# A decoder layer's tiles at other places in SBUF: split tiles 128 bytes longer, x sums and mixer weights 64 bytes into theirs, everything 32 bytes further on, and four small changes of order

## The chip, the cores and the metric

One core of a Trainium2 chip runs the whole layer in one launch. The metric is the device time of one execution in microseconds; where several runs of a kernel are compared, their median. A profiled execution gives the trace; its span is the time from the first to the last instruction.

## The reference

One decoder layer on a sequence of 512 tokens with 1,024 channels, all in float32 (batch 1, depth 1):

```python
x = x + 0.5 * rms_norm(swiglu_ffn(rms_norm(x, norm_pre[0]), ffn1_w_in, ffn1_w_out), norm_post[0])
mixed = token_mixer(rms_norm(x, norm_pre[1]), w_mix_in, ..., w_mix_out)   # HGRN2 + mLSTM heads
x = x + rms_norm(mixed, norm_post[1])
x = x + 0.5 * rms_norm(swiglu_ffn(rms_norm(x, norm_pre[2]), ffn2_w_in, ffn2_w_out), norm_post[2])

def swiglu_ffn(x, w_in, w_out):
    gate, up = jnp.split(x @ w_in, 2, axis=-1)
    return (jax.nn.silu(gate) * up) @ w_out          # 1024 -> 2 x 2816 -> 1024
```

The mixer is one projection to 3,592 columns, a causal convolution, two chunked recurrences and an output projection.

## The kernel before

**Split operands.** Every large matmul is done in float32r on operands split in two: `hi` is the operand rounded by a cast, `lo` the rest, and a product is three matmuls (hi·hi, hi·lo, lo·hi) into one PSUM bank. Weights come by DMA into `raw` tiles of 512 KB (queue of SyncE, L182); `split` (L184 to L212) casts one on ScalarE (L195: `hi`), subtracts on VectorE (L197: `lo`) into one of four `w` buffers, and then lets GpSimd add one raw block to another where a later product needs the sum (L209). `feed` (L214) splits ahead until four buffers are filled; the items stand in one list, so ScalarE, VectorE and GpSimd go through the splits in the list's order.

**The first half of each FFN** multiplies x (transposed, tokens as columns) by blocks of W_in in a scheme with seven block products instead of eight: for each of 11 column groups t the products p1 to p7, each 24 matmuls of 256 columns (`prod`, L444; the matmul is L456). p1, p2, p4 and p5 take x blocks as they are, in the tiles `xq`; p3, p6 and p7 take sums of x blocks, in three tiles of tag `s` (`sq`). Here the weights `w` are the stationary operand and the x blocks the moving one. What is done with a finished product is in `after` (L471): additions and silu on VectorE and ScalarE, between PSUM and the tile `hf` (L475, L483 to L489). t=0, and parts of t=1 and 2, are done early, while the other tokens are still being normalised: products c1 to c4 and e1 to e4, list `HEADS` (L41). c1, c3 and c4 use the `s` tiles for split weights before the sums go there (`stay`, L791). `ORDER` (L43 to L48) is the order of all products, written out by hand; it fixes TensorE's order and the list of splits.

**The second half of each FFN**, and the mixer's token-wise projections, are matmuls of 512 columns (`mm3`, L123 to L127): there the weights `w` are the moving operand, and the stationary one is a block of the hidden layer (`hs`, also tag `s`, from `h_tile`, L628; the last one lies in `xq3`) or of x (`xq`, `t_mm`, L719). Other mixer projections have `xq` moving, 256 columns, and `w` stationary (`in_k`, L405, L409; `head_mm`, L414, L419).

**Between the stages.** At the end of the mixer `mix_out1` finishes tokens in four blocks; `ffn_head` (L511) starts the second FFN in between: splits, copies, the transposes of the last blocks (`trans`), and `sums` (L271), which makes the x sums with a chain of small operations on ScalarE and VectorE (L277 for `lo` and subtractions, L278 for `hi`). `behind` holds instructions back until given ones have been issued. `start` (L543) does the same by hand for the first FFN. It begins with `gain_pe` (L101): a norm row is loaded, multiplied with ones on TensorE (L114) and copied to all partitions, while `spin` (L118) issues filler matmuls (3, then 4, then 4) where TensorE would wait.

**Where the tiles lie.** A tile's byte offset in its partition follows from the sizes of those allocated ahead of it (each rounded up to 32 bytes). What matters below is the offset modulo 128:

| tile | offset | modulo 128 |
|---|---|---|
| `nhalf`, 8 constants | 17024 | 0 |
| `xs` | 17056 | 32 |
| `xq0` to `xq3`, 8192 bytes each | 33440 and on | 32 |
| `w`, four of 8192 bytes | 87008 and on | 96 |
| tag `s` (`sq`, `hs`), three of 8192 bytes | 179936 and on | 96 |

Within these tiles the blocks of a matmul begin at multiples of 512 bytes, so the column holds for every operand. The 6,370 matmuls of the program contain, in float32r with 256 columns: 2,592 of `xq` on `w`, 288 of `xq` on weights in `sq`, 1,440 of sums in `sq` on `w`; with 512 columns: 1,008 of `w` on `hs` and 624 of `w` on `xq`.

Of the kernel before, what the change touches and what calls it, by code (L numbers as in the profile page):

```python
# [14 lines left out]
P = 128  # L15
T = 512
# [3 lines left out]
ND = D // P  # L20
NF = FF // P
EPS = 1e-6
RAW, WBUF = 3, 4
PAIRS = NF // 2
HALF = T // 2
KH = ND // 2
# [13 lines left out]
HEAD = 3  # L40
HEADS = [("c1", 0), ("c3", 0), ("c2", 0), ("c4", 0), ("p1", 1), ("e1", 0), ("e3", 0)]  # L41
HEADS += [("e2", 0), ("p1", 2), ("p2", 1), ("e4", 0), ("p2", 2)]
ORDER = HEADS + [(p, 1) for p in ("p7", "p5", "p3", "p6")] + [("p5", 2), ("p7", 2), ("p3", 2), ("p4", 1), ("p6", 2)]  # L43
for _t in range(HEAD, PAIRS):
    if _t == HEAD:
        ORDER += [("p1", _t), ("p3", _t), ("p5", _t), ("p4", _t - 1)] + [(p, _t) for p in ("p7", "p6", "p2")]
    else:
        ORDER += [("p1", _t), ("p4", _t - 1)] + [(p, _t) for p in ("p3", "p5", "p7", "p6", "p2")]  # L48

# [9 lines left out]
class Item:  # L59

    def __init__(self, key, loads, rows=None, adds=(), dst=None):
        self.key, self.loads, self.rows, self.adds, self.dst = key, loads, rows, adds, dst
        self.reads = {key, *(k for pair in adds for k in pair)}


class Layer:
    def __init__(self, ctx, tc, aps):
        self.tc, self.nc = tc, tc.nc  # L70
        self.__dict__.update(aps)
        nc = self.nc
        pool = lambda name, **kw: ctx.enter_context(tc.tile_pool(name=name, bufs=1, **kw))
        self.cp, self.wp, self.sp, self.psp = pool("cp"), pool("wp"), pool("sp"), pool("psp", space=PSUM)
        self.uid, self.hold = 0, ()

        self.ident = self.cp.tile([P, P], F32, name="ident")
        make_identity(nc, self.ident)
        self.nhalf = self.cp.tile([P, 8], F32, name="nhalf")
        nc.gpsimd.memset(self.nhalf, -0.5)  # L80
        self.xs = self.cp.tile([P, NT, D], F32, name="xs")

        self.xq = [self.cp.tile([P, 2, KH, HALF], F32R, name=f"xq{n}") for n in range(4)]
        self.prm = self.cp.tile([P, 36], F32, name="prm")
# [16 lines left out]
    def gain_pe(self, tag, row):  # L101

        nc = self.nc
        g = self.cp.tile([P, D], F32, tag=tag, bufs=1, name=self.nm(tag))
        r = self.hf[0:1, 14:16, :].rearrange("p a t -> p (a t)")
        nc.sync.dma_start(r, row)
        one = self.st("one", P)[:1]
        nc.gpsimd.memset(one, 1.0)
        self.spare = self.ps()
        self.spin(3)  # L110
        for h in range(2):
            ps = self.ps()
            v = slice(512 * h, 512 * h + 512)
            nc.tensor.matmul(ps, one, r[:, v], start=True, stop=True)  # L114
            nc.vector.tensor_copy(g[:, v], ps)
        return g
# [67 lines left out]
    def split(self):  # L184

        nc = self.nc
        it = self.items.popleft()
        raw = self.raw[it.key]
        _, a, b = raw.shape
        w = it.dst() if it.dst else self.wp.tile([P, 2, a, b], F32R, tag="w", bufs=WBUF, name=self.nm("w"))  # L190
        hi, lo = w[:, 0], w[:, 1]
        self.ready.append((w, it.dst is not None))
        rows = it.rows
        if rows is None:
            nc.scalar.copy(hi, raw)  # L195
            yield
            nc.vector.tensor_tensor(lo, raw, hi.bitcast(F32), op=ALU.subtract)  # L197
        else:
            for j in range(a):
                nc.scalar.activation(hi[:, j], raw[:, j], AF.Copy, scale=rows[:, j : j + 1])  # L200
            yield
            for j in range(a):
                nc.vector.scalar_tensor_tensor(
                    lo[:, j], raw[:, j], rows[:, j : j + 1], hi[:, j].bitcast(F32), op0=ALU.mult, op1=ALU.subtract
                )
        with self.behind(*self.hold):
            for out, other in it.adds:
                o, c = self.raw[out], self.raw[other]
                nc.gpsimd.tensor_tensor(o, o, c, op=ALU.add)  # L209
        self.load_due(self.done)  # L210
        self.done += 1
        yield  # L212

    def feed(self, most=WBUF):  # L214

# [55 lines left out]
    def sums(self, i, src):  # L271


        nc = self.nc
        v = slice((i % 2) * P, (i % 2 + 1) * P)
        f = [x[:, :, v] for x in self.xf]
        sub = lambda out, a, b: nc.vector.tensor_tensor(out, a, b, op=ALU.subtract)  # L277
        hi = lambda dst, src: nc.scalar.copy(dst[:, 0, :, v], src)  # L278
        lo = lambda dst, src: sub(dst[:, 1, :, v], src, dst[:, 0, :, v].bitcast(F32))
        p1, p0 = self.turn(src, 1), self.turn(src, 0)  # L280
        a22 = self.hf[:, 10 + i, :].rearrange("p (c t) -> p c t", c=KH)
        s1, s2, s3, s4 = self.xq[2], self.sq[2], self.sq[1], self.sq[0]
        hi(self.xq[2], p0)
        hi(self.xq[3], p1)
        nc.scalar.copy(a22, p1)
        lo(self.xq[2], p0)
        lo(self.xq[3], p1)
        yield
        sub(p1, p0, a22)
        sub(p0, f[0], p0)  # L290
        hi(s3, p0)
        lo(s3, p0)
        yield
        sub(p0, f[0], p1)
        hi(s1, p1)
        lo(s1, p1)
        yield
        hi(s2, p0)
        sub(p1, f[1], p0)
        lo(s2, p0)  # L300
        yield
        hi(s4, p1)
        lo(s4, p1)
        yield
# [127 lines left out]
    def open_ffn(self, ctx):  # L432

        hp = self.hpool = ctx.enter_context(self.tc.tile_pool(name=self.nm("hp"), bufs=1))
        self.hf = hp.tile([P, NF, T], F32, name=self.nm("hf"))
        self.xf = [self.hf[:, j : j + 2, :].rearrange("p a (b t) -> p (a b) t", t=HALF) for j in (NF - 4, NF - 2)]
        self.sq = [hp.tile([P, 2, KH, HALF], F32R, tag="s", bufs=3, name=self.nm("sq")) for _ in range(3)]
        self.left = {"p1": self.xq[0], "p2": self.xq[1], "p4": self.xq[3], "p5": self.xq[2], "p6": self.sq[2], "p7": self.sq[1], "p3": self.sq[0]}
        self.left.update({"c1": self.xq[0], "c2": self.xq[1], "c3": self.xq[0], "c4": self.xq[1]})
        self.left.update({"e1": self.xq[2], "e2": self.xq[3], "e3": self.xq[2], "e4": self.xq[3]})  # L440
        self.gs, self.held, self.copies = [], {}, []
        self.hs, self.bank, self.later, self.n, self.q, self.had = deque(), {}, deque(), {}, {}, set()
# [68 lines left out]
    def ffn_head(self, trans):  # L511
# [10 lines left out]
        with self.behind(*norm):  # L522
            for g in self.copies:
                next(g)
            self.feed()
        S = lambda: [next(g) for g in self.gs]
        then = {("e1", 0): S, ("e3", 0): S, ("e2", 0): S, ("e4", 0): S}
        for n, (p, t) in enumerate(HEADS):
            self.feed()
            self.lag()  # L530
            self.prod(p, t)
            self.after(p, t)
            if n == 0:
                with self.behind(*norm):
                    trans(2)
            elif n == 2:
                trans(3)
            elif (p, t) in then:
                then[p, t]()
# [3 lines left out]
    def start(self, norm, xn):  # L543
# [2 lines left out]
        norm(1)  # L546
        q = [[self.part(i, h, xn[i]) for h in range(2)] for i in range(2)]
        step = lambda *gs: [next(g) for g in gs]
        self.spin(4)
        step(q[0][0], q[0][1], q[0][0])  # L550
        self.spin(4)
        split = self.split()
        step(q[1][0], q[1][1])
        next(split)
# [72 lines left out]

    def h_tile(self, k2, dst=None):  # L628

        t = dst if dst is not None else self.hpool.tile([P, 2, 2, T], F32R, tag="s", bufs=3, name=self.nm("hs"))  # L630
        src = self.hf[:, 2 * k2 : 2 * k2 + 2, :]
        self.nc.scalar.copy(t[:, 0], src)
        self.nc.vector.tensor_tensor(t[:, 1], src, t[:, 0].bitcast(F32), op=ALU.subtract)  # L633
        return t
# [106 lines left out]
    def mix_items(self):  # L741
# [2 lines left out]

        def item(src, a, b, rows=None):
            key = ("mix", len(made))
            made.append(Item(key, [Load(key, src, a, b)], rows))

        def f(c0):
            for n in range(4):  # L750
# [14 lines left out]
    def ffn_items(self, name, w_in, w_out):  # L765
# [26 lines left out]
        for p, t in ORDER:  # L792
            if p[0] == "e":
                continue
            dst = (lambda n=stay[p]: self.sq[n]) if p in stay else None
            made.append(Item((name, t, place[p]), own.get((p, t), ()), None, adds.get((p, t), ()), dst))
        for h in range(2):
            for k2 in range(PAIRS):
# [585 lines left out]
def layer(tc, aps):  # L1384
    with ExitStack() as ctx:
# [26 lines left out]
        with ExitStack() as f1:  # L1412
            L.open_ffn(f1)
            with tc.manual_schedule():
                first = L.start_loads()
                for i in range(NT):
                    for h in range(2):
                        v = slice(512 * h, 512 * h + 512)
                        (nc.scalar if i == 1 else nc.sync).dma_start(L.xs[:, i, v], x[0, i * P : (i + 1) * P, v])
                        if i == h == 0:  # L1420
                            gp[0] = L.gain_pe("gpre", pre[0:1, :])
                    if i:
                        L.load(first.popleft())
                    if i == 1:
# [44 lines left out]
```

## Time and profile before

| | us |
|---|---|
| median of 3 runs | 976.48 (976.01 to 976.50) |
| the profiled execution | 976.29 |
| its span | 974.6 |
| TensorE busy | 960.6 |
| VectorE busy | 695.0 |
| ScalarE busy | 464.0 |
| GpSimd busy | 291.5 |

The profile's page lists busy time of the engines (PE is TensorE's matmuls, PEld its weight loads, DVE VectorE, ACT ScalarE, POOL GpSimd, SP SyncE), the chain of work that ended last, and groups of instructions by line: output<-inputs, shape, count, busy time and mean ns of one, then the idle time before them and what ended it. A timeline row gives start, duration from the first start to the last end, engine, line, tiles and count; in square brackets stands the idle time just before and what released it. The granted clock of TensorE is 0.997 in the mean. By stages: up to 14 us the start, to 92 us the first products, the first FFN to 374 us, the mixer to 627 us, the second FFN to 968 us, then the last norm and the stores.

### The profile page before, as it was taken

The numbers are of one execution on the slowest core, as the hardware profiler recorded it, in microseconds if no ns is written. First come the engines' busy times: TensorE is split into PE (matmuls) and PEld (weight loads), VectorE is DVE, ScalarE is ACT, GpSimd is POOL, SyncE is SP. The second block draws the span as 40 slices with busy tenths as digits, with TensorE's granted clock in tenths as the row PEclk, the third lists the DMA queues.
The fourth block names the chain that finished last, engine by engine and source line by source line (L and its number), as shares of the span: only waits on it lengthen the run. The fifth ranks groups of instructions, "written<-read, shape, count | busy, mean of one in ns | idle before, by whom it ended". The sixth has DMA issues, their size and how long they took to land.

```text
span 974.6 us, 15937 instructions
## 1 busy us (share of the span) xinstructions
PE 960.6 (99%) x6595; PEld 884.9 (91%) x6595; DVE 695.0 (71%) x796; ACT 464.0 (48%) x625; POOL 291.5 (30%) x224
## 2 busy tenths in 40 slices
PE   8999999999999999999999999999999999999997
PEld 7999999999888889998887888899999999988885
DVE  5798888898545466697846564797988889854543
ACT  6644444445435356955622444564444444543531
POOL 3346555642000036200001210454565565200001
PEclk9999999999999999999999999999999999999999
DMA  9243334335322016321222126114332433233202
GB/s 317 74 130 109 109 90 129 109 109 151 108 100 95 1 25 172 90 85 44 66 65 66 44 82 214 37 58 130 108 110 88 128 110 108 88 109 101 94 1 87
DMA packets 81666, 95.98 MB, mean 98 GB/s; under 512 B 4117, under 2 KB 61497, under 8 KB 81594
## 3 DMA queue, kind: packets, MB, share of 16 engines
q1 hardware_dynamic: 81306, 94.44, 30.7%
q8 instruction: 52, 0.85, 0.4%
q10 hardware_dynamic: 288, 0.52, 0.2%
q14 instruction: 20, 0.16, 0.1%
HBM read 92.85 MB, written 2.10 MB: 97 GB/s over the span
## 4 chain that ended last, share of the span: by engine, by line
PE 91%; DVE 3%; issue 2%; POOL 2%; ACT 1%; DMA 1%; DVEq 0%; POOLq 0%; SPq 0%; ACTq 0%
PE ps L456 38%; PE ps L125 13%; PE ps L127 13%; PE ps L126 13%; PE ps L409 6%; PE ps L969 2%; POOL raw L209 2%; PE ps L419 1%; PE ps L244 1%; DVE w L197 1%; PE ps L1143 0%; ACT w L195 0%; DVE ps L277 0%; PE ps L114 0%; PE ps L1054 0%
## 5 line engine op out<-in xcount | busy, mean ns | idle before, releaser
L197 DVE TENSOR_TENSOR w<-raw,w 128x1024 fp32r<-128x1024 f32 x214 | 341.5, 1608 | 151.7 <-ACT w L195 151.0
L195 ACT CAST w<-raw 128x1024 fp32r<-128x1024 f32 x214 | 224.1, 1052 | 290.3 <-PE ps L127 116.5
L209 POOL TENSOR_TENSOR raw<-raw,raw 128x1024 f32<-128x1024 f32 x80 | 221.2, 2766 | 187.2 <-DVE w L197 170.2
L456 PE MATMUL ps<-xq,w 128*128 128x256 f32 x2016 | 239.9, 278 | 2.6 <-DVE hf L475 2.6
L456 PEld LDWEIGHTS ps<-xq,w 128*128 128x128 f32 x2016 | 235.3, 189 | 3.3 <-ACT w L195 2.3
L456 PE MATMUL ps<-sq,w 128*128 128x256 f32 x1440 | 178.9, 283 | 0.0
L456 PEld LDWEIGHTS ps<-sq,w 128*128 128x128 f32 x1440 | 174.9, 191 | 0.0
L127 PE MATMUL ps<-w,hs 128*128 128x512 f32 x336 | 131.0, 390 | 0.0
L125 PE MATMUL ps<-w,hs 128*128 128x512 f32 x336 | 130.9, 390 | 0.0
L126 PE MATMUL ps<-w,hs 128*128 128x512 f32 x336 | 130.8, 389 | 0.0
L125 PE MATMUL ps<-w,xq 128*128 128x512 f32 x208 | 84.8, 408 | 0.1
L126 PE MATMUL ps<-w,xq 128*128 128x512 f32 x208 | 81.6, 392 | 0.0
L127 PE MATMUL ps<-w,xq 128*128 128x512 f32 x208 | 81.5, 393 | 0.0
L127 PEld LDWEIGHTS ps<-w,hs 128*128 128x128 f32 x336 | 63.1, 188 | 13.6 <-DVE hs L633 0.7
L126 PEld LDWEIGHTS ps<-w,hs 128*128 128x128 f32 x336 | 63.1, 188 | 13.0
L125 PEld LDWEIGHTS ps<-w,hs 128*128 128x128 f32 x336 | 63.1, 188 | 12.9
L330 POOL TENSOR_SCALAR col<-col 128x1 f32<-128x1 f32 x24 | 9.7, 404 | 199.4 <-ACT junk L329 199.2
L409 PE MATMUL ps<-xq,w 128*128 128x256 f32 x480 | 56.5, 278 | 0.0
L409 PEld LDWEIGHTS ps<-xq,w 128*128 128x128 f32 x480 | 55.5, 188 | 0.0
L633 DVE TENSOR_TENSOR hs<-hf,hs 128x1024 fp32r<-128x1024 f32 x42 | 51.1, 1218 | 0.0
L125 PEld LDWEIGHTS ps<-w,xq 128*128 128x128 f32 x208 | 39.1, 188 | 9.0 <-ACT xq L250 0.8
L127 PEld LDWEIGHTS ps<-w,xq 128*128 128x128 f32 x208 | 39.0, 188 | 8.8 <-DVE xq L251 0.2
(230 smaller groups left out, 975.7 us busy)
## 6 DMA issues: line engine op xcount, KB each, us to landing
raw<-in_ffn_w_in_dram SPq DMA_DIRECT2D x88, 512.0 KB, 4.0
raw<-in_ffn_w_out_dram SPq DMA_DIRECT2D x44, 512.0 KB, 3.5
raw<-in_w_mix_in_dram SPq DMA_DIRECT2D x28, 512.0 KB, 3.8
raw<-in_w_mix_out_dram SPq DMA_DIRECT2D x8, 512.0 KB, 3.5
out_dram<-xs SPq DMA_DIRECT2D x8, 256.0 KB, 2.1
xs<-in_x_dram SPq DMA_DIRECT2D x6, 256.0 KB, 6.3
gpost<-in_norm_post_dram SPq DMA_DIRECT2D x3, 512.0 KB, 3.9
gpre<-in_norm_pre_dram SPq DMA_DIRECT2D x2, 512.0 KB, 4.2
```

The source lines that it names most:

```text
L125: mm(ps, sh, mh, start=start, stop=False, **kw)
L126: mm(ps, sh, ml, start=False, stop=False, **kw)
L127: mm(ps, sl, mh, start=False, stop=stop, **kw)
L195: nc.scalar.copy(hi, raw)
L197: nc.vector.tensor_tensor(lo, raw, hi.bitcast(F32), op=ALU.subtract)
L209: nc.gpsimd.tensor_tensor(o, o, c, op=ALU.add)
L244: self.nc.tensor.transpose(pt[:, c * P : (c + 1) * P], src[:, k * P : (k + 1) * P], self.ident)
L409: mm(ps[:, u0:u1], w[:, a, k, :], self.xop(k, b, u0, u1), start=k + n + m == 0, stop=k == ND - 1 and n == 2, skip_group_check=True,)
L419: self.nc.tensor.matmul(ps[:, :HALF], w[:, a, k, :], self.xop(k, b, 0, HALF), start=m + k == 0, stop=m == 2 and k == ND - 1)
L456: self.nc.tensor.matmul(ps[:, c], w[:, b, k, v], left[:, d, k, :], start=first and a + n + k == 0, stop=n == 2 and k == KH - 1, skip_group ...
L633: self.nc.vector.tensor_tensor(t[:, 1], src, t[:, 0].bitcast(F32), op=ALU.subtract)
L969: nc.tensor.matmul(sc[:, 64 * m : 64 * m + 64], k8[:, m], q8[:, m], start=True, stop=True)
```

## The change

Layout: `w` and `s` tiles get 32 more float32 (`PAD`, 128 bytes, so their distances stay multiples of 128); a view placed by `place` begins at the tile's start, or 64 bytes later with `late`. Late are the x sums (`self.sq`) and the split mixer weights with 512 columns (`b == 512`); not late are all other weights, the c weights in `s` tiles (`self.stay`) and the hidden layer (`h_tile`). `nhalf` gets 16 instead of 8 constants, so that all tiles allocated after it lie 32 bytes further on. Afterwards, modulo 128: `xq` at 64, `w` at 0 (mixer weights of 512 columns at 64), sums at 64, weights and `hs` in tag `s` at 0.

Order: p1 of t=3 stands ahead of p6 of t=2 in `ORDER` (both FFNs); the head of the second FFN splits two items and not as many as fit, and from its fifth product on feeds only behind the last `lo` of x; the norm row is the first load of all, and the second halves of the first two blocks of x go through ScalarE's queue; the fillers are 2, 3 and 2.

```diff
-RAW, WBUF = 3, 4
+RAW, WBUF, PAD = 3, 4, 32
...
-ORDER = HEADS + [(p, 1) for p in ("p7", "p5", "p3", "p6")] + [("p5", 2), ("p7", 2), ("p3", 2), ("p4", 1), ("p6", 2)]
+ORDER = HEADS + [(p, 1) for p in ("p7", "p5", "p3", "p6")] + [("p5", 2), ("p7", 2), ("p3", 2), ("p4", 1), ("p1", 3), ("p6", 2)]
...
-        ORDER += [("p1", _t), ("p3", _t), ("p5", _t), ("p4", _t - 1)] + [(p, _t) for p in ("p7", "p6", "p2")]
+        ORDER += [("p3", _t), ("p5", _t), ("p4", _t - 1)] + [(p, _t) for p in ("p7", "p6", "p2")]
...
-        self.nhalf = self.cp.tile([P, 8], F32, name="nhalf")
+        self.nhalf = self.cp.tile([P, 16], F32, name="nhalf")
...
-        self.spin(3)
+        self.spin(2)
...
-        w = it.dst() if it.dst else self.wp.tile([P, 2, a, b], F32R, tag="w", bufs=WBUF, name=self.nm("w"))
+        if it.dst:
+            w = it.dst()
+        else:
+            w = self.place(self.wp.tile([P, 2 * D + PAD], F32R, tag="w", bufs=WBUF, name=self.nm("w")), a, it.late)
...
+    def place(self, t, a, late=False):
+        o = PAD // 2 if late else 0
+        return t[:, o : o + 2 * D].rearrange("p (b k t) -> p b k t", b=2, k=a)
...
-        lo(self.xq[3], p1)
+        self.lowed = lo(self.xq[3], p1)
...
-        self.sq = [hp.tile([P, 2, KH, HALF], F32R, tag="s", bufs=3, name=self.nm("sq")) for _ in range(3)]
+        sq = [hp.tile([P, 2 * D + PAD], F32R, tag="s", bufs=3, name=self.nm("sq")) for _ in range(3)]
+        self.sq = [self.place(t, KH, True) for t in sq]
+        self.stay = [self.place(t, KH) for t in sq]
...
-            self.feed()
+            for _ in range(2):
+                self.full_split()
...
-            self.feed()
+            if n > 3:
+                with self.behind(self.lowed):
+                    self.feed()
...
-        self.spin(4)
+        self.spin(3)
         step(q[0][0], q[0][1], q[0][0])
-        self.spin(4)
+        self.spin(2)
...
-        t = dst if dst is not None else self.hpool.tile([P, 2, 2, T], F32R, tag="s", bufs=3, name=self.nm("hs"))
+        t = dst
+        if t is None:
+            t = self.place(self.hpool.tile([P, 2 * D + PAD], F32R, tag="s", bufs=3, name=self.nm("hs")), 2)
...
-            made.append(Item(key, [Load(key, src, a, b)], rows))
+            made.append(Item(key, [Load(key, src, a, b)], rows, late=b == 512))
...
+                gp[0] = L.gain_pe("gpre", pre[0:1, :])
                 for i in range(NT):
                     for h in range(2):
...
-                        (nc.scalar if i == 1 else nc.sync).dma_start(L.xs[:, i, v], x[0, i * P : (i + 1) * P, v])
-                        if i == h == 0:
-                            gp[0] = L.gain_pe("gpre", pre[0:1, :])
+                        (nc.scalar if i < 2 and h else nc.sync).dma_start(L.xs[:, i, v], x[0, i * P : (i + 1) * P, v])
```

More of the change, by code (lines that the diff above doesn't have):

```diff
@@ L59, with __init__ @@
 class Item:
-    def __init__(self, key, loads, rows=None, adds=(), dst=None):
-        self.key, self.loads, self.rows, self.adds, self.dst = key, loads, rows, adds, dst
+    def __init__(self, key, loads, rows=None, adds=(), dst=None, late=False):
+        self.key, self.loads, self.rows, self.adds, self.dst, self.late = key, loads, rows, adds, dst, late
         self.reads = {key, *(k for pair in adds for k in pair)}
@@ L794, in ffn_items @@
                 continue
-            dst = (lambda n=stay[p]: self.sq[n]) if p in stay else None
+            dst = (lambda n=stay[p]: self.stay[n]) if p in stay else None
             made.append(Item((name, t, place[p]), own.get((p, t), ()), None, adds.get((p, t), ()), dst))
```

## The prediction

> **What bounds the kernel now.** I read the page from the top: the busy shares, then the chain that ended last.
>
> ```profile
> span 974.6 us, 15937 instructions
> ...
> PE 960.6 (99%) x6595; PEld 884.9 (91%) x6595; DVE 695.0 (71%) x796; ACT 464.0 (48%) x625; POOL 291.5 (30%) x224
> ...
> PE 91%; DVE 3%; issue 2%; POOL 2%; ACT 1%; DMA 1%; DVEq 0%; POOLq 0%; SPq 0%; ACTq 0%
> ```
>
> TensorE is busy for 99% of the span and makes up 91% of the chain, so two things can shorten the run: matmuls that follow each other more closely, and the few places where TensorE stands still. A busy TensorE need not be at its best pace, so next come the groups by line.
>
> ```profile
> L456 PE MATMUL ps<-xq,w 128*128 128x256 f32 x2016 | 239.9, 278 | 2.6 <-DVE hf L475 2.6
> ...
> L456 PE MATMUL ps<-sq,w 128*128 128x256 f32 x1440 | 178.9, 283 | 0.0
> ```
>
> Same line, same shape, same weight tiles `w`; only the moving operand differs (`xq` or the x sums in `sq`), and the sums are 5 ns slower on each of 1,440. Mean durations overlap in a pipeline, so the pace is read from starts, in the timeline of TensorE alone in a stretch without any wait.
>
> ```profile
> 104.41 3.02 PE L456 MATMUL ps<-sq,w 128*128 128x256 f32 x24
> 107.27 2.90 PE L456 MATMUL ps<-xq,w 128*128 128x256 f32 x24
> 110.00 5.90 PE L456 MATMUL ps<-sq,w 128*128 128x256 f32 x48
> 115.75 8.34 PE L456 MATMUL ps<-xq,w 128*128 128x256 f32 x72
> 123.92 3.02 PE L456 MATMUL ps<-sq,w 128*128 128x256 f32 x24
> ```
>
> From start to next start, 72 sums take 2.86 + 5.75 us, 119.6 ns each; 96 of `xq` take 2.73 + 8.17 us, 113.5 ns each. What distinguishes them is where the operands lie. Counted modulo 128 bytes, `w` begins at 96, `xq` at 32 and the sums at 96: the slow pair is 0 apart, the fast pair 64. The 512-column matmuls show the other sign:
>
> ```profile
> 567.61 0.39 PE L126 MATMUL ps<-w,xq 128*128 128x512 f32 x1
> ...
> 571.73 0.39 PE L126 MATMUL ps<-w,xq 128*128 128x512 f32 x1
> ...
> 880.10 0.39 PE L127 MATMUL ps<-w,hs 128*128 128x512 f32 x1
> ...
> 885.54 0.39 PE L127 MATMUL ps<-w,hs 128*128 128x512 f32 x1
> ```
>
> 18 matmuls against `xq` (64 apart) take 4.12 us, 228.9 ns each; 24 against `hs` (0 apart) take 5.44 us, 226.7 ns each.
>
> **The change part by part.** The sum is made against the profiled execution, 976.29 us (span 974.6), which is 0.19 us below the median 976.48.
>
> *Layout.* The sums move 64 bytes, so all 4,320 matmuls of 256 columns on `xq` or sums against `w` or `sq` weights are 64 apart. The mixer's 512-column weights move 64 bytes too, so 576 of the 624 `w`-`xq` matmuls become 0 apart (the other 48, on the last h tile in `xq3`, stay 64 apart), and the 1,008 on `hs` stay 0 apart. Everything is also 32 bytes further on: before, every one of these operands begins 32 bytes past a multiple of 64; afterwards, on one. No row shows that position.
>
> The value of distance: the groups say 5.0 ns per sum, the starts 6.1; I take 5.6, between them. Seven products of 24 sums run before the stop that ends at 86 us, where another chain sets the pace (below), so 1,440 - 168 = 1,272 count: x 5.6 ns = 7.1 us. In the mixer, 576 x 2.2 ns = 1.3 us.
>
> The value of position has to be bounded from both sides. The closest pace of a full-width matmul in the trace is that of the transposes, in the chain:
>
> ```profile
> 26.32 0.87 PE ps L244 x8
> ```
>
> 0.87 / 8 = 109 ns. If position let every 256-column matmul reach it: 4,320 x 4.5 = 19.4 us less; 512 columns at twice that, 218 ns, 1,632 x 8.7 = 14.2 us less. On the other side, if it put all 256-column matmuls into the slow pace: 4,320 x 6.1 = 26.4 us more. I take zero: distance is what the two pairs of groups differ in, and a common shift leaves every distance as it was. [...]
>
> *p1 of t=3 ahead of p6 of t=2.* It fills, or not, the longest stop after the start.
>
> ```profile
> 74.87 5.79 POOL L209 TENSOR_TENSOR raw<-raw,raw 128x1024 f32<-128x1024 f32 x2 [1.16 <-DVE w L197]
> 78.22 1.05 ACT L195 CAST w<-raw 128x1024 fp32r<-128x1024 f32 x1 [7.97 <-POOL raw L209]
> 79.30 2.44 DVE L197 TENSOR_TENSOR w<-raw,w 128x1024 fp32r<-128x1024 f32 x1 [2.77 <-ACT w L195]
> ...
> 81.67 0.68 DVE L475 TENSOR_TENSOR n<-ps,hf 128x512 f32<-128x512 f32 x1
> ...
> 85.23 0.68 DVE L475 TENSOR_TENSOR hf<-q,ps 128x512 f32<-128x512 f32 x1
> ...
> 86.06 4.43 PE L456 MATMUL ps<-xq,w 128*128 128x256 f32 x24 [2.14 <-DVE hf L475]
> ```
>
> Read upwards: p4 of t=2 waits 2.14 us for `hf` at L475; that stands on VectorE behind weight splits, whose cast waited 7.97 us for a GpSimd sum, which is queued behind p6's sum. With p1's split first, p1's sum comes first and the cast is free about one sum (2.4 us) earlier. The orders of TensorE, ACT and VectorE move by this one product. p6 itself ends one product later (2.85 us), but p3 and p5 still stand between it and p4. The stop also cools the clock: the 24 matmuls at 86.06 take 4.43 us instead of 2.90. I count the 2.14 and 1.5 us, 3.6 in all; next late are p4's operands in the shorter stop near 69 us, which I leave unchanged.
>
> *Head of the second FFN.* Two splits instead of a full feed, later splits only behind the last low part of x.
>
> ```profile
> 635.76 5.70 DVE L197 TENSOR_TENSOR w<-raw,w 128x1024 fp32r<-128x1024 f32 x3
> ...
> 643.89 1.28 DVE L277 TENSOR_TENSOR xq<-ps,xq 128x512 fp32r<-128x512 f32 x2
> 644.63 4.80 PE L456 MATMUL ps<-xq,sq 128*128 128x256 f32 x40 [1.32 <-DVE xq L277]
> ```
>
> TensorE waits 1.32 us for a low part queued behind three splits (5.70 us). Those go behind it; -1.3 us. The new wait holds ACT's casts and everything after them in its queue, and the p1 products then need their weights: at worst the 1.3 us come back. The first products use weights split earlier, which is the cover.
>
> *Start.* The norm row is loaded first, halves of x go through two queues, and eleven filler matmuls (3, 4 and 4) become seven (2, 3 and 2).
>
> ```profile
> 1.24 3.22 DMA hf<-in_norm_pre_dram
> 4.50 3.78 PE ps L114 x4
> 8.28 2.01 PE ps L121 x8
> 10.28 1.71 PE ps L244 x8
> 11.99 1.06 PE ps L121 x8
> ```
>
> The chain begins with that row. Issued 0.45 us sooner (the x load ahead of it on SP goes), it takes that off all that follows. The fillers of 11.99 to 13.05 cover a wait of which half is real; two fewer give up to 0.5 us. [...] I take 0.6 us.
>
> The scheduler also issues the post-norm row's 512 KB one place earlier on SP, ahead of three weight loads.
>
> ```profile
> 18.68 4.00 SPq L182 DMA_DIRECT2D raw<-in_ffn_w_in_dram  x3
> ...
> 25.51 0.36 SPq L98 DMA_DIRECT2D gpost<-in_norm_post_dram  x1
> ```
>
> SP stands before 18.68 us waiting for VectorE, so the issue itself is free, and the weights of those three are not split before other products have run; at worst they land one 512 KB load later. Nothing is counted for it.
>
> Sum: 7.1 + 1.3 + 3.6 + 1.3 + 0.6 = 13.9; 976.3 - 13.9 = 962.4, and with the 0.2 to the median **962.6 us**. The longer tiles move no work and change no instruction of ACT, VectorE or GpSimd.
>
> **Does VectorE hold it back?** Its busy time in the second FFN, and TensorE's:
>
> ```profile
> 650.00:830.00 180.00, 179.99 (x1549) 179.82 (x1549) 157.15 (x137) 82.43 (x96) 93.57 (x34) 1.00 0.34 106
> ```
>
> 157 of 180 us (third pair); with 663 sums (3/7 of 1,549) x 5.6 = 3.7 us off, 157 of 176. There is room, but order matters in its queue; half of the 7.1 us lost to it would be 966.
>
> **The rivals.**
>
> *Position helps* (0.15). Both bounds above: 962.6 - 33.6 = 929.0 in full, about 946 by half. For it: 113.5 and 226.7 ns lie above 109 and 218, so something still costs 4 to 5%, and all operands begin off a multiple of 64. Against: no row shows one that doesn't.
>
> *Position hurts* (0.21): slower. [...] All 256-column matmuls at 119.6 ns: 962.6 + 26.4 = 989.0. It decides from 13.9 us, that is 3.2 ns on each of 4,320, an average of 116.7 ns. For it: `xq` and sums differ in position as well as in distance, so position alone may have made the pace. Against: for the 512-column pair the moving `w` begins at 96 both times, and the pace still changes with where the stationary one lies.
>
> *Distance does nothing* (0.08). The layout terms vanish: 962.6 + 8.4 = 971.0. [...] The trace speaks against it: 119.6 and 113.5 ns for one shape and the same weights.
>
> **How the numbers follow.** The forecast, 957 to 967, has 0.56: zero for position, with each small step possibly failing. The rivals have 0.15, 0.21 and 0.08. A measurement can tell about 0.2% from no change (974.5 to 978.4). Faster: 0.56 + 0.15 + 0.08 and 0.03 of "hurts" in its mild form, 0.82; same: 0.04, again "hurts"; slower: 0.14. The range 938 to 980 leaves out about 0.07 below (position helping nearly in full) and 0.11 above.
>
> **What would show it.** Sums right: in the timeline, runs of 24 on `sq,w` as long as those on `xq,w`, 2.90 instead of 3.02 us. Mixer right: 226.7 ns from start to start. Position zero: `xq,w` still at 113.5; lower or higher than that, one of the first two rivals, and the forecast is wrong by 4,320 times the difference. Order right: no wait for `hf` near 84 us and no half-speed matmuls after it. Head right: no wait for `xq` at L277 near 643 us. Start right: the first product of L456 before 13.6 us (14.16 now).

## The result, and the profile after

The changed kernel takes **981.76 us** (median of 4 runs, 981.29 to 983.70) against 976.49 of the kernel before (4 runs, 976.01 to 977.14): ratio 1.0057, 95% interval 1.0040 to 1.0075. It is 5.3 us slower; the forecast was 962.6, faster.

The page of the changed kernel, lines as in the prediction (its L466 is L456 of before, L200 is L197, L212 is L209, L485 is L475, L285 is L277):

```profile
span 979.5 us, 15914 instructions
...
PE 965.0 (99%) x6587; PEld 885.5 (90%) x6587; DVE 703.3 (72%) x796; ACT 464.0 (47%) x625; POOL 291.1 (30%) x224
...
PE 87%; DVE 7%; issue 2%; ACT 1%; POOL 1%; DMA 0%; DVEq 0%; POOLq 0%; ACTq 0%
...
L466 PE MATMUL ps<-xq,w 128*128 128x256 f32 x2016 | 243.9, 280 | 5.1 <-DVE hf L485 5.1
...
L466 PE MATMUL ps<-sq,w 128*128 128x256 f32 x1440 | 174.6, 279 | 0.0
```

TensorE is still the bound. The mean of the sums fell by 4 ns (283 before), that of `xq,w` rose by 2 (278 before), and the waits for `hf` doubled (2.6 before). The paces, again from starts in TensorE's timeline:

```profile
104.96 2.99 PE L466 MATMUL ps<-sq,w 128*128 128x256 f32 x24
107.79 2.99 PE L466 MATMUL ps<-xq,w 128*128 128x256 f32 x24
110.61 5.82 PE L466 MATMUL ps<-sq,w 128*128 128x256 f32 x48
116.27 8.54 PE L466 MATMUL ps<-xq,w 128*128 128x256 f32 x72
124.64 2.88 PE L466 MATMUL ps<-sq,w 128*128 128x256 f32 x24
127.36 2.88 PE L466 MATMUL ps<-xq,w 128*128 128x256 f32 x24
```

24 sums take 2.83 us (117.9 ns each), then 24 of `xq` 2.82 (117.5): sums and `xq` alike, at a pace that the trace of before did not show in this stretch. Then, from 124.64, 24 sums take 2.72 us, 113.3 ns, and the 24 of `xq` behind them 113.3 as well. One layout, two paces.

The 512-column matmuls of `w` on `hs`, which kept their distance modulo 128, change pace in the middle of the stage. Three rows, all L127, the first two 15 matmuls apart, the last two 24:

```profile
880.41 0.39 PE L127 MATMUL ps<-w,hs 128*128 128x512 f32 x1
...
883.81 0.40 PE L127 MATMUL ps<-w,hs 128*128 128x512 f32 x1
...
889.40 0.40 PE L127 MATMUL ps<-w,hs 128*128 128x512 f32 x1
```

3.40 / 15 = 226.7 ns, then 5.59 / 24 = 232.9 ns. Counted in a window of 100 us in the last stage (window, sum, TensorE busy and matmuls, clock, DMA share, GB/s), first before, then after:

```profile
860.00:960.00 100.00, 100.00 (x442) 1.00 0.20 69
```

```profile
860.00:960.00 100.00, 100.00 (x436) 1.00 0.20 69
```

Where the time went, from the starts of the same matmul in both traces (the same one by its number, counted back from the last): the first product of L466 is 1.88 us early, the product behind the stop at 86 us 0.34 late, the first matmul of the first FFN's second half (235.60 us before) 0.6 late, the mixer's first 2.4, the second FFN's first 3.3, the first of its second half 3.5, the last matmul 5.1. The 512-column halves of the FFNs lose most (1.8 and 1.5 us), the mixer 0.9; behind the stop the 256-column halves lose 0.2 to 0.3 us each; the start's gain is lost again in the stop at 86 us:

```profile
76.20 0.69 DVE L485 TENSOR_TENSOR ps<-ps,n 128x512 f32<-128x512 f32 x1
...
79.70 2.42 POOL L212 TENSOR_TENSOR raw<-raw,raw 128x1024 f32<-128x1024 f32 x1 [1.16 <-DVE w L200]
80.14 3.05 DVE L200 TENSOR_TENSOR w<-raw,w 128x1024 fp32r<-128x1024 f32 x1
82.15 1.99 ACT L198 CAST w<-raw 128x1024 fp32r<-128x1024 f32 x2 [1.58 <-POOL raw L212]
83.12 0.68 DVE L485 TENSOR_TENSOR n<-ps,hf 128x512 f32<-128x512 f32 x1
...
85.57 0.68 DVE L485 TENSOR_TENSOR hf<-q,ps 128x512 f32<-128x512 f32 x1
...
86.40 4.58 PE L466 MATMUL ps<-xq,w 128*128 128x256 f32 x24 [4.23 <-DVE hf L485]
```

The wait is 4.23 us (2.14 before), the slowed matmuls stay (4.58 us for 24, at a mean granted clock of 0.62 from 86.0 to 90.5 us, 0.65 there before). In both traces the clock granted is 0.5 for 3.41 us (86.82 to 90.23 us, before 87.31 to 90.72), behind a wait of 4.23 us as behind one of 2.14; that the stop is what lowers it is the author's inference. The cast no longer waits 7.97 us for GpSimd, but `n` still stands behind a split whose cast waits for a GpSimd sum, only another one.

The start and the head of the second FFN, also after:

```profile
12.28 3.90 PE L466 MATMUL ps<-xq,sq 128*128 128x256 f32 x32
...
639.01 5.70 DVE L200 TENSOR_TENSOR w<-raw,w 128x1024 fp32r<-128x1024 f32 x3
...
647.15 1.28 DVE L285 TENSOR_TENSOR xq<-ps,xq 128x512 fp32r<-128x512 f32 x2
...
647.89 4.37 PE L466 MATMUL ps<-xq,sq 128*128 128x256 f32 x36 [0.96 <-DVE xq L285]
```

The first product is 1.88 us earlier. At the head the same three splits, 5.70 us, stand ahead of the low part of x; the wait is 0.96 us for 1.32.

### The profile page after: what moved, and what is told of

It reads as the page before. It is cut to its first block, busy times and chain, and to the rows that moved or that the text cites. A ratio compares the mean times of both kernels' runs of the same rounds, so it can differ in the third digit from the quotient of the medians.

```text
span 979.5 us, 15914 instructions
## 1 busy us (share of the span) xinstructions
PE 965.0 (99%) x6587; PEld 885.5 (90%) x6587; DVE 703.3 (72%) x796; ACT 464.0 (47%) x625; POOL 291.1 (30%) x224
## 4 chain that ended last, share of the span: by engine, by line
PE 87%; DVE 7%; issue 2%; ACT 1%; POOL 1%; DMA 0%; DVEq 0%; POOLq 0%; ACTq 0%
PE ps L466 35%; PE ps L125 13%; PE ps L127 13%; PE ps L126 13%; PE ps L417 6%; DVE w L200 4%; PE ps L984 2%; PE ps L252 1%; PE ps L427 1%; DVE hf L485 1%; DVE ps L285 0%; PE ps L1158 0%; ACT w L198 0%; PE ps L1069 0%; PE ps L114 0%
## 5 line engine op out<-in xcount | busy, mean ns | idle before, releaser
L200 DVE TENSOR_TENSOR w<-raw,w 128x1024 fp32r<-128x1024 f32 x214 | 350.8, 1650 | 149.9 <-ACT w L198 149.7
L198 ACT CAST w<-raw 128x1024 fp32r<-128x1024 f32 x214 | 223.9, 1050 | 290.6 <-PE ps L127 119.3
L212 POOL TENSOR_TENSOR raw<-raw,raw 128x1024 f32<-128x1024 f32 x80 | 221.2, 2767 | 188.4 <-DVE w L200 171.4
L466 PE MATMUL ps<-xq,w 128*128 128x256 f32 x2016 | 243.9, 280 | 5.1 <-DVE hf L485 5.1
L466 PEld LDWEIGHTS ps<-xq,w 128*128 128x128 f32 x2016 | 239.3, 189 | 5.8 <-issue 5.6
L466 PE MATMUL ps<-sq,w 128*128 128x256 f32 x1440 | 174.6, 279 | 0.0
L466 PEld LDWEIGHTS ps<-sq,w 128*128 128x128 f32 x1440 | 171.0, 188 | 0.0
L127 PE MATMUL ps<-w,hs 128*128 128x512 f32 x336 | 132.0, 393 | 0.0
L127 PE MATMUL ps<-w,xq 128*128 128x512 f32 x208 | 81.6, 393 | 0.0
L127 PEld LDWEIGHTS ps<-w,hs 128*128 128x128 f32 x336 | 63.1, 188 | 14.7 <-DVE hs L648 0.5
L417 PE MATMUL ps<-xq,w 128*128 128x256 f32 x480 | 56.7, 279 | 0.0
L417 PEld LDWEIGHTS ps<-xq,w 128*128 128x128 f32 x480 | 55.7, 188 | 0.0
L338 POOL TENSOR_SCALAR col<-col,col 128x1 f32<-128x1 f32 x24 | 10.9, 454 | 122.9 <-ACT junk L337 122.6
L125 PEld LDWEIGHTS ps<-w,xq 128*128 128x128 f32 x208 | 39.2, 188 | 9.1 <-ACT xq L258 0.8
```

The source lines that it names most:

```text
L125: mm(ps, sh, mh, start=start, stop=False, **kw)
L127: mm(ps, sl, mh, start=False, stop=stop, **kw)
L338: nc.gpsimd.tensor_scalar(m, ss, s2 / D, b, op0=ALU.mult, op1=ALU.add)
L417: mm(ps[:, u0:u1], w[:, a, k, :], self.xop(k, b, u0, u1), start=k + n + m == 0, stop=k == ND - 1 and n == 2, skip_group_check=True,)
L466: self.nc.tensor.matmul(ps[:, c], w[:, b, k, v], left[:, d, k, :], start=first and a + n + k == 0, stop=n == 2 and k == KH - 1, skip_group ...
```

## The experiments

Each was measured in turns with the kernel before on the same chip; before's median in each set of runs stands beside it. Paces are means over all starts of a kind in the trace of the profiled execution.

### First theory: the position (32 bytes further on) hurts. Rival: the edits of order

**e1_no_shift**, from the changed kernel:

```diff
-        self.nhalf = self.cp.tile([P, 16], F32, name="nhalf")
+        self.nhalf = self.cp.tile([P, 8], F32, name="nhalf")
```

> The changed kernel with the tile of constants back at 32 bytes: x sums, weights and x keep their 64-byte distances, but all lie 32 bytes past a multiple of 64 again, and all edits of order stay. Theory (the position, not the distance, cost the time): sums return from 116.9 ns from start to start to about 114 (1,440 x 2.9 = 4.2 us), xq against w from 116.0 to 113.9 (2,016 x 2.1 = 4.2), w against hs from 230.5 to 226.7 (1,008 x 3.7 = 3.7), the mixer from 230 to 227 (576 x 3 = 1.7): 981.8 - 13.8 = 968, between 965 and 971. Rival (edits of order and the longer stop at 86 us cost the time, the layout nothing): 980 to 983, and paces as in the changed kernel.

Measured: 983.09 us (before 976.85), ratio 1.0067 (1.0054 to 1.0079). Sums 117.0 ns, `xq,w` 116.5, `hs` 230.5: nothing came back. The last stage:

```profile
860.00:960.00 100.00, 100.00 (x436) 1.00 0.22 72
```

**e2_shift_alone**, from the kernel before, the other way round (8 to 16 constants).

> The kernel before with only the tile of constants 32 bytes longer: same orders, same distances, everything after it 32 bytes further on. Theory (position): xq against w leaves 113.9 ns for about 116 (2,016 x 2.1 = 4.2 us), w against hs 226.7 for 230.5 (3.7 us), the sums, 0 apart, stay between 117 and 120: 976.5 + 8 = 984, between 980 and 988. Rival (orders): 976.5, within 1 us. The forecast's own zero for position: 976.5 as well.

Measured: 977.37 us (before 976.85), ratio 1.0003 (0.9994 to 1.0012). TensorE's timeline has the durations of before:

```profile
105.02 3.02 PE L456 MATMUL ps<-sq,w 128*128 128x256 f32 x24
107.88 2.90 PE L456 MATMUL ps<-xq,w 128*128 128x256 f32 x24
110.62 5.90 PE L456 MATMUL ps<-sq,w 128*128 128x256 f32 x48
```

A common shift of 32 bytes does nothing here (3.02 and 2.90 us for 24, as before). The first theory falls, and the forecast's zero for position stands.

**e3_order_alone**, from the changed kernel (no address differs from before):

```diff
-RAW, WBUF, PAD = 3, 4, 32
+RAW, WBUF, PAD = 3, 4, 0
...
-        self.nhalf = self.cp.tile([P, 16], F32, name="nhalf")
+        self.nhalf = self.cp.tile([P, 8], F32, name="nhalf")
...
-        o = PAD // 2 if late else 0
+        o = 0
```

> The kernel before with the order, the head and the start edits, and no change of any address. Theory (position cost the time): the start gives about 1.9 us, the stop near 84 us takes about 2.2 back, so 976.5 within 1.5 us. Rival (orders cost the time): 980 to 983. The forecast's own step values (3.6 + 1.3 + 0.6): 971.

Measured: 978.86 us (before 976.85), ratio 1.0019 (1.0010 to 1.0028): 2.0 us slower, paces as before. Between the two theories: the edits of order cost, but less than half of it.

**e4_layout_alone**, the changed kernel with the old `ORDER`, head and start (those lines of the change undone).

> The changed kernel with the old order, head and start: sums 64 bytes later and everything 32 bytes further on. Theory (position): the paces of the changed kernel, so 976.5 + 4.7 = 981, between 979 and 983.5. Rival (orders cost the time, the layout is worth nothing or a gain): 968 to 977.

Measured: 982.83 us (before 976.85), ratio 1.0060 (1.0047 to 1.0073): 6.0 us slower, paces as in the changed kernel. So the layout costs the time, but neither its shift nor its distances modulo 128 explain it, for `hs` kept both its distance and, in e1, its position. What is left is the length: tiles of 8,320 bytes in place of 8,192.

### Second theory: the distance counts modulo 256 bytes

8,320 is 32 x 256 + 128. Every second buffer of `w` and of tag `s` therefore lies 128 bytes off, modulo 256. Before, all buffers are 8,192 bytes apart, and each kind of pair has a single distance. Stationary minus moving operand, modulo 256: before, sums 0, `xq,w` 64, `hs` 0, mixer 192; after, sums and `xq,w` 64 and 192, `hs` 0 and 128, mixer 0 and 128. By these addresses the changed kernel's own trace already tells distance from place: in `w` on `hs`, modulo 256, `w` and `hs` both at 0 take 227.7 ns and both at 128 take 227.6, while `w` at 0 with `hs` at 128 takes 232.9 and the other way round 232.8.

**f1_len256_late64** and **f2_len256_late192**, from the changed kernel; f1 as shown, f2 with `48` in place of `16`:

```diff
-RAW, WBUF, PAD = 3, 4, 32
+RAW, WBUF, PAD = 3, 4, 64
...
-        o = PAD // 2 if late else 0
+        o = 16 if late else 0
```

> The changed kernel with tiles 256 bytes longer in place of 128, the x sums and the mixer's weights still 64 bytes later. Theory (the distance counts modulo 256 bytes, and a tile 128 bytes longer puts every second pair of buffers 128 bytes off): all hs pairs are 0 apart again, 226.8 ns (1,008 x 3.7 = 3.7 us less than the changed kernel), all xq,w pairs 64, 114 ns (2,016 x 2 = 4.1 us less), but all sums 192 apart, at 117.4 or more (1 us more), and the mixer 128 apart, 232 (1.2 us more): 976, between 974 and 979. Rival (period 128, or nothing but order and early stops): as the changed kernel, 981 to 983.5.

> The run before it (tiles 256 bytes longer) with x sums and mixer weights 192 bytes later in place of 64: modulo 128 the same distances, modulo 256 the sums 64 apart like xq, the mixer 0 apart like hs. Theory (period 256): sums at 114 ns (1,440 x 3 = 4.3 us less than the changed kernel), mixer 226.8 (1.7 less), hs 3.7 and xq,w 4.1 less: 981.8 - 13.8 = 968, between 965 and 971. Rival (period 128): the same time as the run with 64 bytes, within 1 us.

Measured: f1 980.72 us (before 976.70), ratio 1.0033 (1.0021 to 1.0045); f2 977.38 us, ratio 1.0000 (0.9987 to 1.0014), its 12 runs spread from 972.99 to 979.46. The period is 256: alike modulo 128, the two differ by 3.3 us, and the 512-column paces tell 0 from 128: `hs` 226.8 and 226.9 as expected, mixer 232.5 (f1, 128 apart, as expected) and 228.4 (f2, 0 apart, where 226.8 was expected). A longer period is not needed: in f1 every second buffer lies 256 bytes off modulo 512, and pairs alike modulo 256 agree within 0.3 ns (`hs` 227.0 and 226.7, mixer 232.4 and 232.5). The window of the last stage in f1:

```profile
860.00:960.00 100.00, 100.00 (x442) 1.00 0.20 71
```

But both miss their times, f1 by 1.7 us above its upper bound and f2 by 9 us. The paces are those of the profiled executions, 978.18 us in f1 and 979.46 in f2. With 256 columns f1 obeys (sums 117.8, `xq,w` 114.1), and f2 does not: all pairs 64 apart, sums 116.1, `xq,w` 116.0. Its timeline:

```profile
105.66 2.88 PE L466 MATMUL ps<-sq,w 128*128 128x256 f32 x24
108.38 2.88 PE L466 MATMUL ps<-xq,w 128*128 128x256 f32 x24
111.10 5.60 PE L466 MATMUL ps<-sq,w 128*128 128x256 f32 x48
116.54 8.56 PE L466 MATMUL ps<-xq,w 128*128 128x256 f32 x72
124.95 2.99 PE L466 MATMUL ps<-sq,w 128*128 128x256 f32 x24
...
209.75 5.82 PE L466 MATMUL ps<-sq,w 128*128 128x256 f32 x48
215.40 8.80 PE L466 MATMUL ps<-xq,w 128*128 128x256 f32 x72
224.04 2.88 PE L466 MATMUL ps<-sq,w 128*128 128x256 f32 x24
226.76 2.88 PE L466 MATMUL ps<-xq,w 128*128 128x256 f32 x24
```

From 105.66 to 116.54 every matmul takes 113.3 ns (2.72 / 24), sums too: the forecast's hope, come true. Within the next 72 the pace changes to 117.7 and stays there for 99 us (at 209.75: 5.65 / 48), and within the 72 at 215.40 it changes back. In the trace's starts, the changes lie at two pairs of matmuls that came late, by 60 and 80 ns at 121.9 us and by 160 and 80 ns at 220.9 us, both where p4 begins. Lateness alone doesn't decide it: behind a wait of 0.32 us at 697.56 us the pace stays 113.3, and behind another late pair at 811 us it stays 117.8.

**f3_longer_alone**, the kernel before with `PAD` 32 and nothing late (from the changed kernel: e4's edits, `nhalf` 8, `o = 0`).

> The kernel before with the weight and sum tiles 128 bytes longer and nothing else: the sums not moved, nothing shifted by 32 bytes, orders as before. Theory (period 256): hs half at 128, 230.5 ns (3.7 us more), xq,w half at 192, 116 ns (4.1 more), the mixer half at 64 (0.5 to 1 more), the sums half at 0 (119.5) and half at 128, of which no row tells the pace, 114 to 120 (0 to 4 us less): 981 to 986. Rival (the length does nothing, the moved sums cost the time): 976 to 978.

Measured: 984.63 us (before 976.70), ratio 1.0080 (1.0067 to 1.0093), within the theory's bounds. The length alone costs 7.9 us, more than the whole change. `hs` runs at 227.8 where it is 0 apart and at 232.8 where it is 128 apart; sums at 119.6 (0) and 118.8 (128); `xq,w` at 114.6 (64) and 116.6 (192).

**f4_late192_old_order**, f2 with the old `ORDER`:

```diff
-("p4", 1), ("p1", 3), ("p6", 2)]
+("p4", 1), ("p6", 2)]
...
-        ORDER += [("p3", _t), ("p5", _t), ("p4", _t - 1)] + [(p, _t) for p in ("p7", "p6", "p2")]
+        ORDER += [("p1", _t), ("p3", _t), ("p5", _t), ("p4", _t - 1)] + [(p, _t) for p in ("p7", "p6", "p2")]
```

> The run with 192 bytes, and p6 of t=2 ahead of p1 of t=3 again as in the kernel before; start and head edits stay. Theory (that swap lengthened the stop near 86 us by some 2.2 us and cools the clock as long): 2 to 3 us less than the run with 192 bytes and the new order, so 965.5, between 963 and 968, better than both kernels. Rival (the longer stop comes of the start edit, which brings TensorE there 1.9 us earlier, while VectorE, GpSimd and the loads are no sooner): the stop stays 4.2 us and the time that of the run with 192 bytes, within 1 us.

Measured: 974.67 us (before 976.70), ratio 0.9974 (0.9965 to 0.9984), 2.7 us less than f2: the difference is as expected, the time itself is not, since f2's was not. The wait for `hf` at 84 us is 1.97 us for 4.73 in f2's profiled execution, so the rival (the stop stays) falls. `xq,w` at 117.0, sums 117.1: the profiled execution (976.17 us) was in the slower pace for four fifths of its 156 products.

### Third theory: at a distance of 64 two paces hold, and slow sums had kept TensorE in the better one

In the kernel before, the sums at 0 (120 ns) stand between the products of `xq`, and after each run of them `xq` starts again at 114 and goes on at 113.3. With all at 64 no such run stands between. The changed kernel has both paces at 192 too: the two runs of `xq` at 107.79 and 127.36 us above are both 192 apart and take 117.5 and 113.3 ns.

**g1_reset_p3**, from f4:

```diff
-        self.sq = [self.place(t, KH, True) for t in sq]
+        self.sq = [self.place(t, KH, o) for t, o in zip(sq, (0, 48, 48))]
```

with `place` taking the offset itself.

> The run with 192 bytes and the old order, but the sum tile of p3 put back 0 apart from the weights, the other two staying 64 apart. Theory (two paces, 113.3 and 117.7 ns, hold at the one distance of 64 bytes; a short wait throws TensorE into the slower one, where it stays, and a run of sums at 0 throws it back): p3's 480 sums 119.5 ns, all other 256-column matmuls again near 114, so xq,w 2,016 x 2.4 = 4.8 us less, 960 sums x 3.1 = 3.0 less, 480 x 2.4 = 1.2 more than the run that it is cut from: 974.7 - 6.6 = 968, between 966 and 971. Rival (117.7 ns comes of something that goes on beside, VectorE, GpSimd or loads): p3 only slower, 976, and xq,w at 116.6 as before.

Measured: **969.05 us** (before 977.50), ratio 0.9915 (0.9902 to 0.9929), within the theory's bounds, and the rival falls. One sum tile put back in a slow place, and the ratio falls from f4's 0.9974 to 0.9915:

```profile
102.78 3.04 PE L465 MATMUL ps<-sq,w 128*128 128x256 f32 x24
105.65 2.90 PE L465 MATMUL ps<-xq,w 128*128 128x256 f32 x24
108.39 5.60 PE L465 MATMUL ps<-sq,w 128*128 128x256 f32 x48
113.83 8.32 PE L465 MATMUL ps<-xq,w 128*128 128x256 f32 x72
121.99 3.02 PE L465 MATMUL ps<-sq,w 128*128 128x256 f32 x24
124.85 2.90 PE L465 MATMUL ps<-xq,w 128*128 128x256 f32 x24
```

p3's 24 sums are slow (2.87 us from start to start), everything behind them until the next p3 runs at 113.3 to 114. Over the trace: p3's sums 119.3, the other sums 113.5, `xq,w` 114.0 ns. The return itself stands in the second FFN:

```profile
660.29 2.99 PE L465 MATMUL ps<-sq,w 128*128 128x256 f32 x24
663.12 2.99 PE L465 MATMUL ps<-xq,w 128*128 128x256 f32 x24
665.95 5.77 PE L465 MATMUL ps<-sq,w 128*128 128x256 f32 x48
671.56 2.88 PE L465 MATMUL ps<-xq,w 128*128 128x256 f32 x24
```

Sums at 64 and `xq` take 2.83 us for 24 (117.8 ns) until p3 comes at 665.95; in these 48, the 24 of p3 take 119.7 ns, the 24 of p6 behind them 114.2, and the `xq` that follow 113.3. No wait stands there.

**g2, g3, g4** put other distances in the same place: `(56, 40, 8)`, `(16, 16, 16)` and `(60, 32, 24)` in the line above.

> The same with the three sum tiles 32 (p3), 224 (p6) and 96 (p7) bytes apart from the weights. It measures three more distances. Theory (period 256 with the two paces at 64): a distance with a pace of its own breaks the run of 117.7 like 0 does, so xq,w returns to about 114 and the time to 967 to 973; one without leaves xq,w at 116 and more, 973 to 977. The sums between 113.3 and 120 each; no row tells which.

> The same with all three sum tiles 192 bytes apart, the mixer's weights as in the run with 192 bytes (0 apart from x). Theory: sums 117.8 ns as in the run with 256-byte longer tiles and 64 bytes (1,440 x 0.7 = 1.0 us more than at 64 with both paces), and xq,w back at 114.3 behind them (2,016 x 2.3 = 4.6 us less): 974.7 - 3.6 = 971, between 969 and 973.5. Rival (the 117.7 ns of xq,w come of something beside): 975 to 977.

> The same with the sum tiles 16 (p3), 160 (p6) and 128 (p7) bytes apart. It measures three more distances. Theory: 128 apart near 119 ns as in the kernel with only longer tiles (118.8); 16 near the pace of 0; both throw the pace back, so xq,w at about 114 and 970 to 975 in all. Rival: xq,w at 116 and more, 975 to 978.

Measured, beside the same 977.50: g2 973.31 us, ratio 0.9961 (0.9948 to 0.9973); g3 973.18, 0.9957 (0.9944 to 0.9969); g4 975.11, 0.9978 (0.9969 to 0.9987). `xq,w` is back at 114.4 in g2 and 113.7 in g3, so sums at 192, and the mixed 32, 96 and 224, bring TensorE back, though not each time (in f1 `xq` goes on at 117.6 behind sums at 192 from 836 us on). In g4 it is 115.6, and the expectation that 16 and 128 throw the pace back fails: from 158.55 us, behind a wait, `xq` stays at 117.8 past all three kinds of sums for the 75 us that are left of the half.

```profile
164.26 2.99 PE L465 MATMUL ps<-xq,w 128*128 128x256 f32 x24
167.09 5.92 PE L465 MATMUL ps<-sq,w 128*128 128x256 f32 x48
172.85 8.64 PE L465 MATMUL ps<-xq,w 128*128 128x256 f32 x72
```

g2 and g4 end just above their upper bounds. Sums by distance, in the runs in which each sum tile has one:

| distance | 0 | 16 | 32 | 64 | 96 | 128 | 160 | 192 | 224 |
|---|---|---|---|---|---|---|---|---|---|
| ns | 119.5 | 117.2 | 118.1 | 113.3 or 117.7 | 117.3 | 119.4 | 119.8 | 117.8 | 117.5 |

No distance but 64 has a mean below 117 here, and 64 gives 113.3 when TensorE comes in at that pace. The table is not the whole rule: in the changed kernel some sums 192 apart run at 113.3 as well (p3 of t=7, at 163 us), and why there and not in f1 and g3 stays open.

### Which edit of order failed

Each alone on the kernel before, so with before's paces (lines as in the change): **h1** only `ORDER`, **h2** only the head, **h3** only the start; **h4** is g1 with the old head.

> The kernel before with nothing changed but p1 of t=3 ahead of p6 of t=2. Theory (the swap lengthens the stop near 86 us from 2.3 to about 4.6 us, since the same GpSimd sum stands ahead of the cast, the split and the three L485 pieces, now one product later): 2 to 3 us slower than before, 979.5. Rival, the forecast's step: 3.6 us faster, 973.

> The kernel before with only the edit of the second FFN's head. Theory (the same three splits of 5.7 us still stand ahead of the low part of x, and splits held back later in the head come late in the stage): no gain at 643 us, 0 to 1.5 us slower, 977.5. Rival, the forecast's step: 1.3 us faster, 975.2.

> The kernel before with only the edits of the start: norm row first, x in two queues, four filler matmuls fewer in number of calls. Theory: the first product starts 1.9 us earlier (12.2 in place of 14.16 us) and the early stops give part of it back: 0.5 to 1.9 us faster, 975.3. The forecast's step: 0.6 us faster, 975.9. Rival (the stop near 86 us is set by loads, GpSimd and VectorE, which gain nothing): no change, 976.5.

> The run with p3's sums 0 apart and the others 64, with the head of the second FFN as before: the best of the layouts, the new start, and neither of the other two edits. Theory (the head edit gains nothing): 0 to 1.5 us less than that run's 969.1, so 968.3, between 967 and 970. Rival (the head edit is worth its 1.3 us): 970.4.

Measured, beside 976.70: h1 980.81 us, ratio 1.0037 (1.0024 to 1.0051); h2 976.52, 1.0000 (0.9992 to 1.0009); h3 974.79, 0.9978 (0.9969 to 0.9987); h4 **969.09**, 0.9918 (0.9906 to 0.9931). The first three add up to +4.1 - 0.2 - 1.9 = +2.0 us, which is what e3 measured. TensorE in h1:

```profile
76.72 5.90 PE L466 MATMUL ps<-sq,w 128*128 128x256 f32 x48
82.46 2.90 PE L466 MATMUL ps<-xq,w 128*128 128x256 f32 x24
89.81 4.60 PE L466 MATMUL ps<-xq,w 128*128 128x256 f32 x24 [4.45 <-DVE hf L485]
```

p6 and p3 (48), p5 (24), then p4, which waits 4.45 us. h1 loses more than the 2 to 3 us expected. Between the two profiled executions (spans 4.5 us apart) this stop explains 2.3; losses of 0.5 and 0.3 us at 144 and 715 us are new. Another 1.8 us arise in the first 23 us, where the swap moves nothing: whether they belong to the swap stays open.

## Why the prediction was wrong

**The step that failed** is the first one on layout: "Counted modulo 128 bytes". The period is 256, and the longer tiles, which the forecast counted at nothing ("move no work"), put every second buffer 128 bytes off. The trace of before couldn't have told: with all buffers 8,192 bytes apart each pair had one distance, whatever the modulus, and the distances seen fit either (0 and 64; the mixer's, 64 modulo 128, is 192 modulo 256). The forecast should have taken the length as a change of its own and bounded it.

- *Sums, 7.1 us.* They went from 119.5 to 116.9 ns: 1,440 x 2.6 = 3.7 us. More than half of the pairs (57%) lie at 192, and two paces hold instead of one. The forecast read 113.5 as the pace of a distance; it was the pace of a distance in one order of work. The trace of before had a hint: p4 of t=3 in the second FFN, behind a pair that comes 80 ns late at 711 us, runs at 117.8.
- *`xq,w`, held at 113.5 by the forecast.* 113.9 became 116.0: 2,016 x 2.1 = 4.2 us lost, more than the sums gained.
- *`hs`, 0 by the forecast ("stay 0 apart").* 226.8 became 230.5: 1,008 x 3.7 = 3.7 us lost.
- *Mixer, 1.3 us.* 228.6 at 0, 232.2 at 128, in the mean 230.4 against 229.6 before: 0.5 us lost. What the forecast called 64 apart was 192; at 64 these matmuls take 233.4 (f3).
- *Position, zero.* Right (e2: 977.37 against 976.85 us). The rival "position hurts" came close to the measured time for a wrong reason: slower, but not by the shift.
- *p1 ahead of p6, 3.6 us.* Wrong in sign: 2.7 (f2 to f4, with the two paces mixed in) to 4.1 us (h1, with the unexplained 1.8 at its start) lost. The forecast said that p3 and p5 still stand between p6 and p4. Between p6's sums and p4's `hf` lies a chain of L485 pieces that is just as long as before: from 76.20 to 85.57, 9.4 us, in the rows above, and 9.4 in before, from this row to its `hf` at 85.23:

```profile
75.85 0.69 DVE L475 TENSOR_TENSOR ps<-ps,n 128x512 f32<-128x512 f32 x1
```

  Before, p1, p3 and p5 cover it; afterwards p1 has gone ahead, and one product of cover (2.8 us) is missing. The early cast only met the next GpSimd sum. The 1.5 us counted for the clock did not come back either: 4.58 us for p4's 24 matmuls, 4.43 before.
- *Head, 1.3 us.* Nothing (h2; h4 against g1). The same three splits still stand ahead of the low part of x, as the rows at 639.01 and 647.15 show.
- *Start, 0.6 us.* Right in sign, too small: 1.9 us (h3). The norm row and the fillers came to 0.95 at most, and what takes this down to 0.6 no run shows: in the changed kernel, with fewer fillers, the matmuls of 128 columns pass from 0.21 to 0.11 us from start to start at 11.7 us, at 12.2 before.
- *What would show it.* The forecast's own test, `xq,w` still at 113.5 or else one of the first two rivals, pointed at a wrong cause when it failed: the length was not on the list.
- *VectorE as the bound.* It isn't: g1 gives it the same work and ends 0.85% below before (969.05 against 977.50 us).
- *Distance does nothing* (the third rival). Refuted: 226.7 and 232.9 ns for one kind of matmul in one stage.

The parts do not add up exactly: e4 and e3 cost 6.0 and 2.0 us, the whole change 5.3. In f2 the pace changes at late matmuls (121.9 and 220.9 us), and each edit may move those; whether that makes up the 2.7 us between is not shown.

## What to carry to other kernels

A layout edit that lengthens a buffer changes the distances between all its copies and all that follow; work them out modulo more than one power of two, for every pair of operands that is read together, before counting it as free (here 128 bytes of length cost 7.9 us, f3). A pace read from a trace holds for its whole setting, the matmuls ahead of it included (113.3 and 117.7 ns at the same 64 bytes, f2): ask what could bring TensorE into another one and what would bring it back. And when a product is moved forward, count what it had been covering (a wait of 4.45 us in h1, 2.14 before).

## What the runs showed of the hardware

- Float32r matmuls of 512 columns take 226.8 ns (`hs`) to 228.4 (mixer) where moving and stationary operand lie 0 apart modulo 256 bytes, 229.6 at 192 (before), 232.2 to 232.9 at 128 (after, f1, f3) and 233.4 at 64 (f3). It is the distance and not the place of either operand: moving both by 128 bytes leaves 227.7 and 227.6.
- With 256 columns and 64 bytes between the operands (in the changed kernel also with 192) two paces, 113.3 and 117.7 ns, hold for up to some 800 matmuls in a row. In f2 the changes seen at 121.9 and 220.9 us lie at matmuls that came 60 to 160 ns late; that the lateness is the cause is inferred from that, and other late pairs change nothing. In g1 24 matmuls 0 apart end the slower pace each of the three times that they meet it (at 103, 666 and 710 us); in g4 it goes on for 75 us past matmuls 16, 128 and 160 apart. Why the period is 256 bytes, no run here shows.
- The best place found is not the fastest pair everywhere but one slow run in seven products: 969.1 us, 0.8% below the kernel before. Of these 7.6 to 8.5 us the edits of the start alone are worth 1.9 (h3).
